# adaLN weights requested by ScalarE's queue instead of GpSimd's

## The chip, the cores and the metric

The kernel runs on one core of a Trainium2 chip. The metric is the device time of one execution in microseconds (us); the median of several runs is compared. The engines of the core are TensorE (PE, matmuls; its weight loads are PEld), VectorE (DVE), ScalarE (ACT), GpSimd (POOL) and SyncE (SP). A transfer (DMA) is requested by an instruction of one of these engines and carried by 16 DMA engines that all requests share.

## The reference

One layer of a decoder trunk, in fp32, for T = 320 tokens: 256 of a prompt and 64 of samples (8 sequences of 8 tokens), with 9 conditioning vectors c (one for the prompt, eight for the samples).

```python
mod = silu(c) @ w_ada + b_ada                       # (9, 6*2048): six sections
sh1, sc1, g1, sh2, sc2, g2 = split(mod, 6)
h = rmsnorm(x, norm1_g) * (1 + sc1) + sh1
p = h @ w_in                                        # q, k, v, og, u, ga, gb, alr
mix = gates(gla(q, k, v, alr, state_gla), pool(u, state_pool))
x = x + g1 * (mix @ w_o)
h2 = rmsnorm(x, norm2_g) * (1 + sc2) + sh2
x = x + g2 * ((silu(h2 @ w_gate) * (h2 @ w_up)) @ w_down)
y = rmsnorm(x, final_norm_g)                        # and new states of gla and pool
```

The adaLN part is the first line: w_ada has 2048 x 12288 fp32 values, 100 MB, and its results scale, shift and gate everything else.

## The kernel before, in words

Every large product is made of three matmuls on split operands (`mm3`, L171 to L173). SyncE loads raw weights in blocks of 512 KB (`raw_chunk`, tile raw, L149, three buffers), ScalarE makes the high part (`split`, tile whi, L157), VectorE the low part (wlo, L158); whi and wlo have four buffers each (WB = 4). Activations are split likewise into hh and hl.

w_ada isn't split. Its blocks are multiplied as they are by the transposed silu(c) (scT), in bursts of 32 or 16 matmuls; a burst's result is copied by ScalarE (tile adasb), transposed on TensorE and added up into mod by VectorE. The stages, in order of time:

- The head (0 to some 200 us). Sections 0 and 1 (shift and scale of h) in 16 blocks of 256 columns. `hada_load` (L225) requests such a block as two pieces of 1 MB into tile hraw (a pool with two buffers), `hada` (L236) is its burst, and the copy is L239. The products with w_in for the first head run in slices of rows between them (SLICES), since a slice needs only the rows of h that are ready. SyncE requests the first two blocks, GpSimd the other 14. Each block's reload waits for the burst that read its buffer two blocks earlier. GpSimd also requests xspill (transposed x put aside).
- The end of the head and the mixer (h = 0 to 3, to about 870 us). Sections 4, 2 and 3 in 24 blocks of the same size: `ada_load` takes the tile araw, `ada_piece` (L269) requests 1 MB, `ada_all` all pieces outstanding, `ada_burst` (L301, copy L310) multiplies. BURST_UNITS and LOAD_UNITS say after which projection of a head a burst or a request is written; araw has one buffer here, so a request waits for the burst before it. GpSimd also requests the states S (L775), writes o_gs (L811) and does small vector work. `anchor` makes a one-column copy (tick) on GpSimd behind which a request is put.
- w_o (some 870 to 1000 us). Eight pieces of section 5 are requested one at a time, each behind GpSimd's product xs (L1016).
- The FFN (to the end). Eight more pieces, requested by GpSimd.

Within an engine the instructions run in the order in which a scheduler placed them when the kernel was built; `high_priority` and `issue_after` are hints to it. `issue_after(x)` places an instruction behind x. The transfers that SyncE and ScalarE request use eight semaphores in turn, those of GpSimd eight others; a request that takes a semaphore waits until the transfer that had it before has landed.

Of the kernel before, what the change touches and what calls it, by code (L numbers as in the profile page):

```python
# [79 lines left out]
def body(tc, A):  # L80
# [57 lines left out]
    more = []  # L138
    last_raw = []
    last_mm = []  # L140

    def raw_chunk(src, nk, nn, pool=None, tag="raw", bufs=3):

# [8 lines left out]
    def split(raw):  # L152
        n = raw.shape[2]
        hi = wp.tile([P, 512 // n, n], F32R, tag="whi", bufs=WB, name=nm("whi"))
        lo = wp.tile([P, 512 // n, n], F32R, tag="wlo", bufs=WB, name=nm("wlo"))
        hi, lo = hi[:, 0:raw.shape[1]], lo[:, 0:raw.shape[1]]
        S.copy(hi, raw)  # L157
        V.tensor_sub(lo, raw, hi.bitcast(F32))  # L158
        return hi, lo

# [59 lines left out]
    def hada_load(sec, b0, pool, eng):  # L220
# [4 lines left out]
            eng.dma_start(t[:, k:k + 8], wada[:, k:k + 8, blk * P:(blk + 2) * P])  # L225
        return t

    def hada(sec, b0, t, pool):

        blk = sec * KT + b0  # L230
        w = 2 * P
        ps = misc()
        with tc.high_priority():
            for r in (3, 2, 1, 0):
                for j in range(4):
                    PE.matmul(ps[32 * j:32 * j + 32, 0:w], lhsT=scT[:, 4 * r + j, :], rhs=t[:, 4 * r + j, :],  # L236
                              start=r == 3, stop=r == 0, tile_position=(0, 32 * j))
        sb = pool.tile([P, w], F32, tag="adasb", name=nm("adasb"))
        S.copy(sb, ps[:, 0:w])  # L239
        pt = misc()  # L240
        for i in range(2):
            tr(pt[:, i * P:(i + 1) * P], sb[:, i * P:(i + 1) * P])
        dst = mod[:, blk:blk + 2, :]
        V.tensor_reduce(dst, pt[:, 0:w].rearrange("p (b j r) -> p b r j", b=2, j=4)[:, :, 0:9, :],
                        axis=AX.X, op=ALU.add)
        bb = bada[:, blk:blk + 2].unsqueeze(2).broadcast_to([P, 2, 9])
        V.tensor_tensor(dst, dst, bb, op=ALU.add)
        if sec == 1:
            V.scalar_tensor_tensor(dst, dst, 1.0, N1G[:, b0:b0 + 2].unsqueeze(2).broadcast_to([P, 2, 9]),
                                   op0=ALU.add, op1=ALU.mult)  # L250
# [8 lines left out]
    ada_want = []  # L259
    ada_ps = []  # L260

    def ada_piece(after=None):

        n, t, r = ada_want.pop(0)
        sec, b, nb, k0, nk = BURSTS[n]
        step = min(nk, 16 // nb)
        col = (sec * KT + b) * P
        with tc.issue_after(after) if after is not None else nullcontext():
            nc.gpsimd.dma_start(t[:, r:r + step], wada[:, k0 + r:k0 + r + step, col:col + nb * P])  # L269

    tick = cp.tile([P, 1], F32, name="tick")

    def anchor(src):

        return G.tensor_copy(tick, src).ins
# [5 lines left out]
            t = ada_raw[n] = apool[0].tile([P, nk, nb * P], F32, tag=tag, bufs=bufs, name=nm("araw"))  # L281
            ada_want.extend((n, t, r) for r in range(0, nk, min(nk, 16 // nb)))

    def ada_all(after=None):
        while ada_want:
            ada_piece(after)

    def ada_burst():

        n = len(ada_done)  # L290
        sec, b, nb, k0, nk = BURSTS[n]
        ada_done.append(n)
        w = nb * P
        if k0 == 0:
            ada_ps[:] = [misc()]
        ps = ada_ps[0]
        first = True
        with tc.high_priority(), tc.issue_after(last_mm[0]):
            for r in range(nk - 4, -1, -4):
                for j in range(4):  # L300
                    PE.matmul(ps[32 * j:32 * j + 32, 0:w], lhsT=scT[:, k0 + r + j, :], rhs=ada_raw[n][:, r + j, :],  # L301
                              start=k0 == 0 and first, stop=k0 + nk == KT and r == 0, tile_position=(0, 32 * j))
                first = False
        if k0 + nk < KT:
            return
        pt = misc()
        for q in range(0, nb, 2):
            wq = min(2, nb) * P
            sb = apool[0].tile([P, wq], F32, tag="adasb", name=nm("adasb"))
            S.copy(sb, ps[:, q * P:q * P + wq])  # L310
            for i in range(wq // P):
                tr(pt[:, (q + i) * P:(q + i + 1) * P], sb[:, i * P:(i + 1) * P])
        blk = sec * KT + b
        V.tensor_reduce(mod[:, blk:blk + nb, :], pt[:, 0:w].rearrange("p (b j r) -> p b r j", b=nb, j=4)[:, :, 0:9, :],
                        axis=AX.X, op=ALU.add)
        if b == KT - nb:
            dst = mod[:, sec * KT:(sec + 1) * KT, :]
            bb = bada[:, sec * KT:(sec + 1) * KT].unsqueeze(2).broadcast_to([P, KT, 9])
            V.tensor_tensor(dst, dst, bb, op=ALU.add)
            if sec == 4:  # L320
                V.tensor_scalar(dst, dst, 1.0, None, op0=ALU.add)
                V.tensor_tensor(dst, dst, N2G.unsqueeze(2).broadcast_to([P, KT, 9]), op=ALU.mult)

    def modp(sec, kt):
        return mod[:, sec * KT + kt, 0:1]
# [97 lines left out]
    with tc.tile_pool(name="head", bufs=1) as xp:  # L423
# [88 lines left out]
        def h_rows(b):  # L512

            def load(s):
                raws[s, b] = hada_load(s, b, xp, nc.gpsimd)
            return ([lambda: load(0), lambda: (h_pre(b), h_pre(b + 1)), lambda: load(1),
                     lambda: hada(0, b, raws.pop((0, b)), xp),
                     lambda: (hada(1, b, raws.pop((1, b)), xp), h_post(b), h_post(b + 1))])
# [7 lines left out]
        for si, (k0, k1) in enumerate(SLICES):  # L526
            last = k1 == KT
            bg = [] if last else [f for b in range(*SLICES[si + 1], 2) for f in h_rows(b)]
            if last:
                with tc.issue_after(spilt[-1]):  # L530
                    walr = xp.tile([P, KT, 16], F32, name="walr")
                    nc.gpsimd.dma_start(walr, win[:, :, OAL:OAL + 16])
                    nc.gpsimd.dma_start(msk, A["ci"])
                    cum = xp.tile([P, NM0 + NM1 + NMS], F32, name="cum")
                    nc.gpsimd.dma_start(cum, A["cf"][:, 64:CFW])
                    nc.gpsimd.dma_start(invc, A["cf"][:, 0:64])
            done = 0
            for ui, (kind, i, col) in enumerate(us):
                want = len(bg) * (ui + 1) // len(us)
                while done < want:  # L540
                    bg[done]()
                    done += 1
                if kind in "qku":
                    evac(proj(win, col, k0, k1, hh, hl), g0, kind, 0, 0 if si == 0 else 1)
                else:
                    for i, ps in enumerate(proj2(win, col, k0, k1, hh, hl)):
                        evac(ps, g0, kind, i, 0 if si == 0 else 1)
                if last and ui == 0:
                    alr_proj(walr, cum)
                if last and ui in (0, 1):  # L550
                    ada_load(ui, 2, "araw")
                    ada_all()
                if last and ui in (2, 3, 5, 6):
                    ada_burst()
                    if ui < 5:
                        ada_load(len(ada_done) + 1, 2, "araw")
                        ada_all()

    apool[0] = acx.enter_context(tc.tile_pool(name="ap", bufs=1, side="right"))

# [384 lines left out]
    for h in range(1, H):  # L945
        pump(RATE)
        g = new_group(h)
        for ui, (kind, i, col) in enumerate(units(h)):
            if kind == "og" and i == 0:
                pump(len(queue))  # L950
                new_gates(g)
            ps = proj(win, col, 0, KT, hh, hl)
            evac(ps, g, kind, i, None)
            if kind == "u":
                pump(len(queue))
                st, E = gla_steps(g)
                pst, psy = pool_steps(g)
                queue += pst + st
            if ui in BURST_UNITS[h]:
                ada_burst()  # L960
            if ui in LOAD_UNITS[h] and len(ada_done) < AMIX:
                ada_load(len(ada_done), 1)
                ada_all(None if ui in BURST_UNITS[h] else anchor((g.q if kind == "q" else g.og)[:, 0, 0:1]))
            pump(RATE)
        queue += psy + [merge_step(g, E)]
    pump(len(queue))
# [41 lines left out]
    for ui in range(8):  # L1008
        ps = proj(wo, 256 * ui, 0, KT, mh, ml, between=x1_rows)
        for i in range(2):  # L1010
            residual(ps, i, 2 * ui + i, 2)
            k = 2 * ui + i
            sq = sq_acc(acc, k, k == 0)
            if k == 12:
                exp_ln_set(sq)
            gi = G.tensor_tensor(s3(xs[:, k]), s3(x1[k][:, TP:T]), mods(4, k), op=ALU.mult).ins  # L1016
            if ada_want:
                ada_piece(gi)

    def rstd_bcast(acc):  # L1020
        pt = misc()
# [31 lines left out]
    for pi, (f0, f1) in enumerate(parts):  # L1053
        ah, al = {}, {}
        for f in range(f0, f1, 2):
# [14 lines left out]
            if pi == 0 and f >= 2:  # L1070
                if f in (4, 8, 12, 16):
                    ada_burst()
                if f in (2, 4, 8, 12):
                    ada_load(len(ada_done), 1)
                    ada_all()
        if pi == 0:
            bcx.close()
        else:
# [67 lines left out]
```

## Time and profile before

| | |
|---|---|
| median of 3 runs | 1975.34 us (1972.93 to 1976.12) |
| the profiled execution | 1972.99 us |
| its span (first to last instruction) | 1971.2 us |
| requests of hraw by GpSimd / SyncE | 28 / 4, 1 MB each, median 9.8 / 11.7 us to landing |
| requests of araw by GpSimd | 64, 1 MB each, median 8.7 us to landing |
| bytes by hardware queues / GpSimd's software queue | 261.81 MB / 136.57 MB |

The profile has a line per engine (busy us, share, instructions), a row of DMA shares in 40 slices of the span, queues with their packets and bytes, the chain of work that ended last, groups of instructions by line, and waits: "ACT whi L157 <- PE ps L172" is time in which ScalarE stood before the cast whi until TensorE's matmul into ps released it. An engine's wait costs only where TensorE, or whatever ends last, waits in turn.

### The profile page before, as it was taken

The page shows a single profiled execution, that of the slowest core. Times are in us where ns is not written, and L with a number is a line of the kernel's source. Part 1 is how long each engine was busy: PE and PEld are TensorE (multiplying, and loading weights), DVE is VectorE, ACT ScalarE, POOL GpSimd, SP SyncE. Part 2 cuts the span into 40 slices and gives each one's busy share as a digit, 9 for nine tenths or more (in the row PEclk, how much of TensorE's full clock was granted, in tenths as well). Part 3 has the DMA queues.
Part 4 walks back from the last instruction along what each step waited for, and adds up shares of the span by engine and source line. Part 5 has one row for each costly group of instructions (what it writes and reads, how often), then busy time and mean ns, then how long its engine had stood idle before and what let it go on. Part 6 is the DMA issues. An engine that isn't in the chain of part 4 may idle for free.

```text
span 1971.2 us, 34613 instructions
## 1 busy us (share of the span) xinstructions
PE 1924.5 (98%) x13808; PEld 1825.2 (93%) x13808; DVE 1007.0 (51%) x1935; ACT 826.9 (42%) x1485; POOL 207.3 (11%) x323
## 2 busy tenths in 40 slices
PE   5999999999999999999999999999999999999997
PEld 4889888988998899989989999999999999999997
DVE  3776454666355535665574444444444444444554
ACT  4433343544345433553354333333333434344443
POOL 2231131221121112111030000000000000000000
PEclk9999989999999999999999999999999999999998
DMA  9996647777875788579845555444545444444442
GB/s 349 354 354 237 203 150 264 219 230 251 256 223 188 247 268 272 183 249 321 269 153 158 186 188 182 145 150 144 156 145 155 150 150 150 150 151 144 149 139 98
DMA packets 287308, 400.60 MB, mean 203 GB/s; under 512 B 11953, under 2 KB 243921, under 8 KB 286809
## 3 DMA queue, kind: packets, MB, share of 16 engines
q1 hardware_dynamic: 250170, 261.81, 42.7%
q0 software_dynamic: 36976, 136.57, 19.5%
q8 instruction: 108, 1.77, 0.4%
q14 instruction: 54, 0.44, 0.1%
HBM read 373.90 MB, written 24.67 MB: 202 GB/s over the span
## 4 chain that ended last, share of the span: by engine, by line
PE 82%; DMA 3%; ACT 1%; DVE 0%; issue 0%; POOL 0%; ACTq 0%; DVEq 0%
PE ps L172 25%; PE ps L171 25%; PE ps L173 25%; PE pm L301 3%; PE pm L135 1%; DMA araw<-w_ada 1%; PE pm L786 1%; PE pm L807 1%; DMA raw<-w_o 1%; DMA S<-state_gla 1%; PE pm L752 1%; DMA o_gs<-S 0%; PE pm L782 0%; PE pm L591 0%; PE pm L741 0%; PE psy L171 0%
## 5 line engine op out<-in xcount | busy, mean ns | idle before, releaser
L158 DVE TENSOR_TENSOR wlo<-raw,whi 128x512 fp32r<-128x512 f32 x952 | 657.7, 694 | 792.4 <-ACT whi L157 779.9
L157 ACT CAST whi<-raw 128x512 fp32r<-128x512 f32 x952 | 587.8, 622 | 948.3 <-PE ps L172 830.1
L171 PE MATMUL ps<-hh,whi 128*128 128x320 f32 x1408 | 441.9, 314 | 6.1 <-ACT hh L337 2.6
L172 PE MATMUL ps<-hl,whi 128*128 128x320 f32 x1408 | 440.4, 313 | 0.0
L173 PE MATMUL ps<-hh,wlo 128*128 128x320 f32 x1408 | 437.4, 312 | 0.0
L172 PE MATMUL ps<-h2l,whi 128*128 128x320 f32 x1408 | 434.7, 309 | 0.0
L171 PE MATMUL ps<-h2h,whi 128*128 128x320 f32 x1408 | 434.7, 309 | 0.0
L173 PE MATMUL ps<-h2h,wlo 128*128 128x320 f32 x1408 | 434.2, 309 | 0.0
L171 PEld LDWEIGHTS ps<-hh,whi 128*128 128x128 f32 x1408 | 265.2, 188 | 19.7 <-issue 9.0
L172 PEld LDWEIGHTS ps<-hl,whi 128*128 128x128 f32 x1408 | 265.3, 188 | 10.4 <-issue 9.4
L173 PEld LDWEIGHTS ps<-hh,wlo 128*128 128x128 f32 x1408 | 264.7, 188 | 8.0 <-issue 5.3
L171 PEld LDWEIGHTS ps<-h2h,whi 128*128 128x128 f32 x1408 | 264.4, 188 | 3.4 <-ACT ah L337 3.4
L172 PEld LDWEIGHTS ps<-h2l,whi 128*128 128x128 f32 x1408 | 264.5, 188 | 0.1
L173 PEld LDWEIGHTS ps<-h2h,wlo 128*128 128x128 f32 x1408 | 264.5, 188 | 0.0
L171 PE MATMUL ps<-ah,whi 128*128 128x320 f32 x704 | 217.7, 309 | 0.0
L172 PE MATMUL ps<-al,whi 128*128 128x320 f32 x704 | 216.5, 308 | 0.0
L173 PE MATMUL ps<-ah,wlo 128*128 128x320 f32 x704 | 216.5, 308 | 0.0
L172 PEld LDWEIGHTS ps<-al,whi 128*128 128x128 f32 x704 | 132.0, 187 | 0.0
L171 PEld LDWEIGHTS ps<-ah,whi 128*128 128x128 f32 x704 | 131.9, 187 | 0.0
L173 PEld LDWEIGHTS ps<-ah,wlo 128*128 128x128 f32 x704 | 131.9, 187 | 0.0
L269 POOL DMA_DIRECT2D araw<-w_ada x64 | 55.1, 864 | 397.2 <-PE pm L301 385.9
L172 PE MATMUL ps<-ml,whi 128*128 128x320 f32 x256 | 79.3, 310 | 0.0
(282 smaller groups left out, 1634.2 us busy)
## 6 DMA issues: line engine op xcount, KB each, us to landing
raw<-w_gu SPq DMA_DIRECT2D x176, 512.0 KB, 3.5
raw<-w_in SPq DMA_DIRECT2D x170, 512.0 KB, 4.4
araw<-w_ada POOLq DMA_DIRECT2D x64, 1024.0 KB, 8.7
raw<-w_down SPq DMA_DIRECT2D x80, 512.0 KB, 3.5
hraw<-w_ada POOLq DMA_DIRECT2D x28, 1024.0 KB, 9.8
S<-state_gla POOLq DMA_DIRECT2D x16, 1024.0 KB, 8.3
o_gs<-S POOLq DMA_DIRECT2D x16, 1024.0 KB, 6.9
raw<-w_o SPq DMA_DIRECT2D x32, 512.0 KB, 6.2
```

The lines of the kernel that those rows point to most:

```text
L135: PE.transpose(out, in_, ident[:k, :k])
L157: S.copy(hi, raw)
L158: V.tensor_sub(lo, raw, hi.bitcast(F32))
L171: PE.matmul(ps, lhsT=whi, rhs=xhi, start=start, stop=False)
L172: PE.matmul(ps, lhsT=whi, rhs=xlo, start=False, stop=False)
L173: last_mm[:] = [PE.matmul(ps, lhsT=wlo, rhs=xhi, start=False, stop=stop).ins]
L269: nc.gpsimd.dma_start(t[:, r:r + step], wada[:, k0 + r:k0 + r + step, col:col + nb * P])
L301: PE.matmul(ps[32 * j:32 * j + 32, 0:w], lhsT=scT[:, k0 + r + j, :], rhs=ada_raw[n][:, r + j, :], start=k0 == 0 and first, stop=k0 + nk == ...
L752: PE.matmul(pt, lhsT=E["kdn"][:, s, d * P:(d + 1) * P], rhs=E["vn"][:, s], start=s == 0, stop=s == 1)
L786: PE.matmul(pt[32 * j:32 * j + 32, :], lhsT=qeP[:, d, 4 * gg + j, :], rhs=E["S0", gg, d][:, j], start=False, stop=d == 0, tile_position=(0 ...
L807: PE.matmul(pt, lhsT=E["kpn"][:, j, d * P:(d + 1) * P], rhs=E["vp"][:, gg], start=True, stop=True)
```

## The change

28 requests of hraw and 56 of araw go from GpSimd to ScalarE; the eight araw requests of the FFN stay. Each is placed behind an instruction of ScalarE: in the head behind the adasb copy of the last burst of the same section (`used`), in the mixer behind the adasb copy of the burst just written (`out`), or the last whi cast (`last_cast`) where no burst goes before, in w_o behind ScalarE's square sq. The four tick copies at those places are gone.

```diff
     def split(raw):
...
-        S.copy(hi, raw)
+        last_cast[:] = [S.copy(hi, raw).ins]
...
+    used = {}
     def hada(sec, b0, t, pool):
...
-        S.copy(sb, ps[:, 0:w])
+        used[sec] = S.copy(sb, ps[:, 0:w]).ins
...
-    def ada_piece(after=None):
+    def ada_piece(after=None, eng=nc.scalar):
...
-            nc.gpsimd.dma_start(t[:, r:r + step], wada[:, k0 + r:k0 + r + step, col:col + nb * P])
+            eng.dma_start(t[:, r:r + step], wada[:, k0 + r:k0 + r + step, col:col + nb * P])
...
-    def ada_all(after=None):
+    def ada_all(after=None, eng=nc.scalar):
         while ada_want:
-            ada_piece(after)
+            ada_piece(after, eng)
     def ada_burst():
...
-            S.copy(sb, ps[:, q * P:q * P + wq])
+            out = S.copy(sb, ps[:, q * P:q * P + wq]).ins
...
+        return out
...
             def load(s):
-                raws[s, b] = hada_load(s, b, xp, nc.gpsimd)
+                with tc.issue_after(used[s]):
+                    raws[s, b] = hada_load(s, b, xp, nc.scalar)
...
                 if last and ui in (0, 1):
                     ada_load(ui, 2, "araw")
-                    ada_all()
+                    ada_all(last_cast[0])
                 if last and ui in (2, 3, 5, 6):
-                    ada_burst()
+                    out = ada_burst()
                     if ui < 5:
                         ada_load(len(ada_done) + 1, 2, "araw")
-                        ada_all()
+                        ada_all(out)
...
+            out = last_cast[0]
             if ui in BURST_UNITS[h]:
-                ada_burst()
+                out = ada_burst()
             if ui in LOAD_UNITS[h] and len(ada_done) < AMIX:
                 ada_load(len(ada_done), 1)
-                ada_all(None if ui in BURST_UNITS[h] else anchor((g.q if kind == "q" else g.og)[:, 0, 0:1]))
+                ada_all(out)
...
-            gi = G.tensor_tensor(s3(xs[:, k]), s3(x1[k][:, TP:T]), mods(4, k), op=ALU.mult).ins
+            G.tensor_tensor(s3(xs[:, k]), s3(x1[k][:, TP:T]), mods(4, k), op=ALU.mult)
             if ada_want:
-                ada_piece(gi)
+                ada_piece(sq)
...
                     ada_load(len(ada_done), 1)
-                    ada_all()
+                    ada_all(None, nc.gpsimd)
```

The scheduler also moves other instructions. ScalarE at the start of the head, before (numbers in names count tiles in the order in which they are written; x2 is two instructions in a row):

```order
L239 COPY adasb_240<-pm_223 128x256
L157 CAST whi_285<-raw_283 128x512
L157 CAST whi_308<-raw_306 128x512
L157 CAST whi_346<-raw_344 128x512
L239 COPY adasb_264<-pm_247 128x256
L482 COPY xT_329<-pm_325 128x320
L482 COPY xT_338<-pm_334 128x320
L337 CAST hh_86<-xh_210 128x320
```

The same place now:

```order
L242 COPY adasb_240<-pm_223 128x256
L226 DMA hraw_302<-w_ada 128x8x256 x2
L158 CAST whi_285<-raw_283 128x512
L158 CAST whi_308<-raw_306 128x512
L158 CAST whi_346<-raw_344 128x512
L242 COPY adasb_264<-pm_247 128x256
L226 DMA hraw_403<-w_ada 128x8x256 x2
L486 COPY xT_329<-pm_325 128x320
L486 COPY xT_338<-pm_334 128x320
L341 CAST hh_86<-xh_210 128x320
```

A pair of requests stands behind each adasb copy, ahead of the casts that TensorE needs next. TensorE in the middle of the head, at the burst of the eleventh block (hraw_1356), before:

```order
L173 MATMUL ps_1001<-hh_91,wlo_1021 128x320
L236 MATMUL pm_1456<-hraw_1356,scT 32x256 x16
L171 MATMUL ps_1062<-hh_90,whi_1066 128x320
L172 MATMUL ps_1062<-hl_106,whi_1066 128x320
L173 MATMUL ps_1062<-hh_90,wlo_1067 128x320
```

The same burst now:

```order
L174 MATMUL ps_899<-hh_91,wlo_903 128x320
L135 MATMUL pm_1302<-cst,adasb_1300 128x128 x2
L135 MATMUL pm_1359<-cst,xn_132 128x128
L135 MATMUL pm_1359<-cst,xn_133 128x128
L135 MATMUL pm_1359<-cst,xn_134 128x128
L135 MATMUL pm_1368<-cst,xn_132 128x128
L135 MATMUL pm_1368<-cst,xn_133 128x128
L135 MATMUL pm_1368<-cst,xn_134 128x128
L239 MATMUL pm_1456<-hraw_1356,scT 32x256 x16
L172 MATMUL ps_937<-hh_90,whi_940 128x320
```

It stood behind the weights whi_1004 to whi_1021 and stands now ahead of whi_940: four blocks of w_in that were multiplied before it come after it. The burst before it (hraw_1234) stays ahead of whi_902 now, and the last of the head, hraw_1911, moved from the second half of whi_1629 to ahead of the second use of whi_1381. GpSimd in the last mixer stage, before:

```order
L811 DMA o_gs<-S_1004_6059 128x4x512
L269 DMA araw_6689<-w_ada 128x8x256 x2
L269 DMA araw_6995<-w_ada 128x8x256 x2
L269 DMA araw_7159<-w_ada 128x8x256 x2
...
L269 DMA araw_7868<-w_ada 128x8x256 x2
L275 COPY tick<-v_7377 128x1
L775 DMA S_1361_8224<-state_gla 128x4x512
L775 DMA S_1362_8226<-state_gla 128x4x512
```

and now:

```order
L816 DMA o_gs<-S_1003_6055 128x4x512
L816 DMA o_gs<-S_1004_6057 128x4x512
L278 COPY tick<-v_7374 128x1
L780 DMA S_1361_8221<-state_gla 128x4x512
L780 DMA S_1362_8223<-state_gla 128x4x512
```

The state loads no longer stand behind seven araw blocks, each of which waits for a burst.

More of the change, by code (lines that the diff above doesn't have):

```diff
@@ L140, in body @@
     last_mm = []
+    last_cast = []
     def raw_chunk(src, nk, nn, pool=None, tag="raw", bufs=3):
```

## The prediction

> **What bounds the kernel now.** I read the page's head first (who is busy), then the chain that ended last, then the busy time by stretches, and only then the waits.
>
> ```profile
> PE 1924.5 (98%) x13808; PEld 1825.2 (93%) x13808; DVE 1007.0 (51%) x1935; ACT 826.9 (42%) x1485; POOL 207.3 (11%) x323
> ...
> DMA  9996647777875788579845555444545444444442
> ...
> q1 hardware_dynamic: 250170, 261.81, 42.7%
> q0 software_dynamic: 36976, 136.57, 19.5%
> ...
> PE 82%; DMA 3%; ACT 1%; DVE 0%; issue 0%; POOL 0%; ACTq 0%; DVEq 0%
> ```
>
> TensorE (PE) is busy for 98% and fills 82% of the chain; DMA has 3% of it. The DMA row says where transfers could matter: the first three slices (0 to 148 us) are full, later ones mostly are not. The next view cuts the span into stretches; its columns are the stretch, busy us of PE, PEld, DVE, ACT and POOL (instructions in brackets), granted clock, DMA share, GB/s.
>
> ```profile
> 0.00:50.00 50.00, 28.25 (x251) 22.81 (x251) 15.32 (x46) 21.51 (x35) 12.86 (x22) 0.97 0.95 349
> 100.00:150.00 50.00, 48.99 (x430) 42.85 (x429) 37.37 (x85) 17.37 (x37) 16.23 (x22) 1.00 0.99 348
> 150.00:200.00 50.00, 48.51 (x343) 45.69 (x342) 28.01 (x53) 15.46 (x28) 4.66 (x8) 1.00 0.66 230
> 700.00:750.00 50.00, 50.00 (x417) 45.50 (x416) 18.58 (x36) 18.51 (x38) 8.33 (x11) 1.00 0.83 269
> 1550.00:1600.00 50.00, 50.00 (x343) 50.00 (x342) 21.88 (x33) 20.11 (x33) 0.00 (x0) 1.00 0.47 148
> 24.00:148.00 124.00, 117.18 (x1048) 100.01 (x1048) 83.01 (x195) 48.52 (x97) 35.85 (x47) 0.99 0.99 365
> 30.00:60.00 30.00, 27.52 (x240) 23.53 (x244) 15.96 (x42) 14.08 (x27) 7.66 (x10) 0.94 1.00 380
> ```
>
> The row at 1550 is TensorE undisturbed: 343 matmuls in 50 us, one each 0.146 us. Where the moved requests act, TensorE loses 21.75 us in the first 50 (start-up, ahead of any moved request but the first two), and then about 1 us in 50: 1.01 at 100, 1.49 at 150, none at 700. A change of the queue cannot win what TensorE does not lose; it can easily make it lose more. That asymmetry carries the forecast.
>
> **The waits the moved requests cause.** Columns: us in total, times, longest.
>
> ```profile
> ACT whi L157 <- PE ps L172: 830.1, 752, 4.7
> POOL araw L269 <- PE pm L301: 385.9, 21, 69.2
> ACT adasb L239 <- PE pm L236: 22.8, 12, 5.9
> POOL S L775 <- DMA o_gs<-S: 15.3, 7, 5.0
> PE pm L236 <- DMA hraw<-w_ada: 0.4, 1, 0.4
> PE pm L301 <- DMA araw<-w_ada: 1.0, 2, 0.5
> PEld pm L301 <- DMA araw<-w_ada: 1.5, 2, 0.8
> PE pm L786 <- DMA S<-state_gla: 0.6, 1, 0.6
> ```
>
> GpSimd (POOL) stands still 385.9 us in front of araw requests, but TensorE, which sets the end, waits only 0.4 us for hraw, 2.5 for araw and 0.6 for a state tile that is requested behind such araw rows: 3.5 us in all. If every one of them goes, that is -3.5; if a wait only changes its place, 0. I take -2.0, nearer to the upper end, since a request on ScalarE (ACT) no longer keeps the state loads waiting, while an araw tile is still released by the same burst of matmuls.
>
> **The issue cost.** How long the engine is held by one 1 MB request, in ns (least, median, most):
>
> ```profile
> L225 POOL DMA_DIRECT2D hraw<-w_ada x28: 882/892/905, 23.8 to 138.3; - x28
> L225 SPq DMA_DIRECT2D hraw<-w_ada x4: 576/3057/4450, 5.6 to 14.1; - x4
> L149 SPq DMA_DIRECT2D raw<-w_in x182: 367/368/2631, 16.9 to 857.3; - x182
> L157 ACT CAST whi<-raw 128x512 fp32r<-128x512 f32 x423 | 259.8, 623 | 412.9 <-PE ps L172 306.6 <-DMA raw<-w_in 36.9 <-DMA raw<-w_o 28.0
> ```
>
> 84 requests (28 hraw, 56 araw) leave GpSimd: 84 x 0.892 = 75 us there, on an engine that waits anyway, so 0. They arrive on ScalarE. No row shows a request of ScalarE, but SyncE (SP) made the same kind through a hardware queue: 0.368 us when the queue has room, 0.576 for the first of four 1 MB blocks, and up to 4.45 when the blocks before it are still in the queue. So 84 x 0.368 to 84 x 0.576 = 31 to 48 us of ScalarE. The last row above is the casts between 32 and 1000 us: ScalarE stood 306.6 us in front of them because TensorE had not yet freed a whi buffer. That is the cover, so 0 on the path. It ends where ScalarE is away longer than the lead of the four whi buffers, whose best witness is the longest of those waits, 4.7 us. A pair that costs 0.576 + 4.45 = 5.03 us overruns it by 0.3; if all 42 pairs did, +14. No such instruction can gain, so the ends are 0 and +14. A new pair meets at most what is left of one older pair in ScalarE's queue, where SyncE's slow ones met three earlier blocks, so I take +0.5. Behind a blocked request stand the casts and hh of the next rows; TensorE waits for those. SyncE's and GpSimd's own queues only get shorter neighbours: the xspill, state and o_gs requests left on GpSimd no longer stand behind 84 requests, which can only bring them forward. One wait is new on SyncE: its raw requests and ScalarE's share the eight semaphores of the hardware queues in turn, so about one raw request in six waits for an hraw or araw to land. In the built order the weights so held back are used 11 to 24 us of TensorE work after the very tile they wait for, so 0; without that distance TensorE would wait a raw's own landing. The four tick copies that drop, and the wait on the adasb copy (0.37 us, in program order on ScalarE itself) are at nothing beside these.
>
> **The request comes when the adasb copy is done,** not when the last matmul is. The row of adasb waits shows ScalarE already standing at that copy in 12 of the 16 head rows, so a request follows a burst by one copy, and 0.892 - 0.576 us of issuing is saved on each half. These cancel: 0.
>
> **The head's cadence** is the larger effect, and the diff doesn't tell it: the scheduler now puts the head's bursts earlier among the matmuls. Durations of one matmul and one burst of 32 (hada), and the last burst:
>
> ```profile
> 154.30 0.31 PE L171 MATMUL ps<-hh,whi 128*128 128x320 f32 x1
> 154.54 1.93 PE L236 MATMUL pm<-hraw,scT 128*32 128x256 f32 x32
> ```
>
> Counting the rows between bursts at 0.147 and 1.93 us, the time from the end of burst n to the start of n+2, in which that tile must be reloaded, was 14.7 to 18.2 us; now it is 11.2 to 16.5. The last burst stands 15.1 us earlier in TensorE's work, so it would start at 154.5 - 15.1 = 139.4, with 2.3 MB less of w_in used by then. The window 24 to 148 moved 365 GB/s x 124 us = 45.3 MB at a DMA share of 0.99; less 2.3 is 43.0 MB, wanted in 139.4 - 24 = 115.4 us: 373 GB/s. At the 365 of that row the transfers end 117.8 us after 24, 2.4 late; at the 380 of the window 30 to 60 they are in time; at the 348 of 100 to 150 they take 123.6 us, 8.2 late. I take +2.4, the row that covers the whole stretch, with ends 0 and +8.2. What is late next is nothing: after the last burst the DMA share falls to 0.66, so what is lost stays lost once and no more.
>
> **The last mixer stage** (h=3) is tighter by the same kind of move: from one burst's end to the next start 11.6 to 12.4 us before, 10.7 now, at a DMA share of 0.83.
>
> ```profile
> L269 POOL DMA_DIRECT2D araw<-w_ada x64: 748/882/987, 149.1 to 1216.4; - x64
> ...
> DMA to landing us min/median/max: 5.8/8.7/11.8
> ```
>
> A pair needs its second request (0.58) and its landing: 9.3 us at the median, in time, and 12.4 at the worst, 1.7 late on six reloads. Ends 0 and +10; I take +0.5, near the median row. Elsewhere in the mixer and in w_o the gaps are 20 us and more or the pieces come singly: 0, with the same landing row as cover.
>
> **Sum:** -2.0 + 0.5 + 0 + 2.4 + 0.5 = +1.4 us. The profiled execution took 1972.99 us (span 1971.2 and 1.8 around it), so 1974.4 by it; it stood 2.35 under the median of 1975.34, so the forecast for the median is 1976.7.
>
> The Trainium skill, "DMA: Bandwidth & Descriptors", section "Issuing engines are not separate DMA queues", speaks against any large gain: transfers from whichever engine share the same 16 DMA engines, and issuing from several saves only sequencer time. The trace agrees as far as it goes, since both queues together fill 0.99 of the DMA share in the head. By the rule alone the sum would be that of the issue term and the waits, between -3.5 and +0.5.
>
> **Rivals.** *Faster:* all 3.5 us of waits go, and so does the 1.49 us TensorE lost between 150 and 200, because the last hraw is out of the way earlier; the head keeps 373 GB/s or more. -5.0: 1970.3. For it: the faster issue. Against: the head's row of 365.
>
> *Slower, the head becomes bound by transfers.* A software packet carried 136.57 MB / 36976 = 3.7 KB, a hardware one 261.81 / 250170 = 1.05 KB. With hraw cut as small as the weights, hraw loses its larger share against raw, or the total rate falls. It decides below 373 GB/s over 24 to 139 us; it costs more than 0.2% (3.95 us) of the kernel below 352 with the other terms at -1.0 (43.0 MB / 0.352 = 122.2, 6.8 late); at 348 it is 8.2 late, and with the pairs in h=3 late by 1 us each on top, 1981.5 to 1986. For it: a share of 0.99 leaves no room, and the reload gaps shrink to 11.2 us against a landing of up to 14.7:
>
> ```profile
> DMA to landing us min/median/max: 7.1/10.2/14.7
> ```
>
> Against: raw landings were the late ones in the head (36.9 us of ScalarE's waits), and they would improve. The Trainium skill, same page, section "Queues, rings and completion order", has each DMA engine take turns between the queue rows packet by packet, by which a queue with smaller packets gets a smaller part; the packet sizes above are this trace's only evidence on it.
>
> *Slower, ScalarE is held by a full queue:* the +14 above, 1989. Against: at most one older pair is in that queue.
>
> *Nothing happens:* the transfers are hidden before and after, and the bursts' earlier places cost nothing: 1975.3.
>
> **From cases to numbers.** The sum as worked out 0.37, nothing 0.14, faster 0.13, head bound by transfers 0.26, ScalarE held 0.10. About 0.2%, 3.95 us, is what a measurement can tell from no change: the first two are within it, the third is faster, both slow cases are slower: 0.13, 0.51, 0.36. The range leaves out some of the fastest end and the queue-held case: 1970.5 to 1986.5. The likeliest case alone has 1973 to 1979.
>
> **What would show it.** Right: rows of ScalarE's hraw and araw requests at 0.37 to 0.6 us, TensorE's waits for araw gone, its idle time between 50 and 150 us up by 2 or 3 us with hraw as releaser. Wrong: such requests above 3 us, whi waits that end in a DMA request rather than in TensorE, a DMA rate in the head under 350 GB/s, or TensorE's idle time falling where no wait stood.

## The result and the profile after

The changed kernel takes 1993.1 us (median of 4 runs, 1991.1 to 1998.1) against 1975.67: a ratio of 1.0092, 95% interval 1.0079 to 1.0106, or 17.4 us slower by the medians (18.2 by the ratio). The forecast was 1976.7 within 1970.5 to 1986.5. The profiled execution has a span of 1991.2 us, 20.0 more than before.

The head of the page after, with the lines that answer to those of before:

```profile
PE 1925.9 (97%) x13808; PEld 1825.3 (92%) x13808; DVE 1010.2 (51%) x1935; ACT 827.8 (42%) x1485; POOL 133.2 (7%) x235
...
q1 hardware_dynamic: 250170, 261.81, 42.4%
q10 hardware_dynamic: 83264, 88.09, 13.2%
q0 software_dynamic: 14128, 48.49, 6.8%
```

The work is the same: 1925.9 us of TensorE against 1924.5, the same megabytes. ScalarE's queue is the new q10, in packets of 88.09 MB / 83264 = 1.06 KB. So the time went into waits. The stretches after (columns as before):

```profile
100.00:150.00 50.00, 42.57 (x397) 34.85 (x397) 33.48 (x80) 15.65 (x34) 6.63 (x11) 1.00 0.99 341
150.00:200.00 50.00, 47.43 (x338) 45.53 (x338) 32.29 (x57) 17.13 (x29) 0.00 (x0) 1.00 0.54 161
24.00:148.00 124.00, 106.19 (x974) 87.58 (x966) 74.12 (x179) 43.49 (x90) 10.93 (x19) 0.96 1.00 347
30.00:60.00 30.00, 22.83 (x199) 18.82 (x198) 13.54 (x38) 11.93 (x24) 2.15 (x4) 0.83 1.00 355
```

Between 24 and 148 us TensorE does 106.19 us of work where it did 117.18: 11 us of the 20 are here. The DMA share is 1.00 (0.99 before), but the rate is 347 GB/s, not 365. The rows of the requests, the waits of TensorE that they bring, a wait of SyncE (SPq) and the last burst of the head:

```profile
L226 ACTq DMA_DIRECT2D hraw<-w_ada x28: 374/529/6405, 25.2 to 138.3; - x28
...
PE ps L172 <- ACT hh L341: 7.0, 1, 7.0
PE pm L304 <- DMA araw<-w_ada: 3.1, 2, 1.7
PE pm L239 <- DMA hraw<-w_ada: 3.0, 3, 1.7
PEld pm L304 <- DMA araw<-w_ada: 2.4, 2, 2.0
...
SPq L150 <- DMA hraw<-w_ada: 11.2, 3, 8.6
...
153.68 1.93 PE L239 MATMUL pm<-hraw,scT 128*32 128x256 f32 x32 [0.76 <-DMA hraw<-w_ada]
```

The median request takes 0.53 us, inside the 0.37 to 0.58 of the forecast, but one takes 6.4 and another 3.8. The last hraw request leaves at 138.3 us, to the tenth where it left before, although its burst stands 15 us earlier in TensorE's order. That burst is the last row: it starts at 153.68, where before it started at 154.54. Moved up 15.1 us in the order, it came 0.9 us sooner, and TensorE stood for the rest. The row above it is new: SyncE's requests for weights stand 11.2 us until an hraw has landed; before there was no such row.

To place the loss I added up, for each TensorE instruction, the time to the next start beyond the median of its kind in the kernel before (bursts, short products and stops of before leave a remainder there too, so only differences count). This count is worked out from the traces of one execution each; the times decide.

| count in us up to | 50 | 250 | 350 | 1000 |
|---|---|---|---|---|
| before | 16.0 | 51.3 | 67.6 | 119.9 |
| after | 20.4 | 61.9 | 83.6 | 140.3 |
| head alone on ScalarE | 20.7 | 64.2 | 79.7 | 134.7 |
| mixer and w_o alone | 15.9 | 50.0 | 69.8 | 126.3 |

### The profile page after: what moved, and what is told of

Same layout as the page of the kernel before. It is cut to its first block, busy times and chain, and to the rows that moved or that the text cites. A ratio compares the mean times of both kernels' runs of the same rounds, so it can differ in the third digit from the quotient of the medians.

```text
span 1991.2 us, 34608 instructions
## 1 busy us (share of the span) xinstructions
PE 1925.9 (97%) x13808; PEld 1825.3 (92%) x13808; DVE 1010.2 (51%) x1935; ACT 827.8 (42%) x1485; POOL 133.2 (7%) x235
## 3 DMA queue, kind: packets, MB, share of 16 engines
q10 hardware_dynamic: 83264, 88.09, 13.2%
## 4 chain that ended last, share of the span: by engine, by line
PE 80%; DMA 3%; ACT 1%; DVE 1%; issue 0%; POOL 0%; ACTq 0%; DVEq 0%; POOLq 0%
PE ps L173 24%; PE ps L172 24%; PE ps L174 24%; PE pm L304 2%; DMA araw<-w_ada 2%; PE pm L135 1%; PE pm L791 1%; PE pm L757 1%; PE pm L812 1%; DMA o_gs<-S 1%; PE pm L746 0%; PE pm L787 0%; PE pm L687 0%; PE pm L596 0%; ACT L106 0%
## 5 line engine op out<-in xcount | busy, mean ns | idle before, releaser
L174 PE MATMUL ps<-mh,wlo 128*128 128x320 f32 x256 | 79.3, 310 | 0.0
```

The lines of the kernel that those rows point to most:

```text
L174: last_mm[:] = [PE.matmul(ps, lhsT=wlo, rhs=xhi, start=False, stop=stop).ins]
```

## The experiments

Theory A: ScalarE is held by requests into its full queue. Theory B: the bursts' earlier places in the head want the transfers sooner than they come. Theory C came later, for the start. Microseconds below are the ratio's excess times 1975, each run against the kernel before as timed in the same session.

### The head alone, and the rest alone

```diff
 # head alone: the kernel before, and
-                raws[s, b] = hada_load(s, b, xp, nc.gpsimd)
+                with tc.issue_after(used[s]):
+                    raws[s, b] = hada_load(s, b, xp, nc.scalar)
 # rest alone: the changed kernel without these lines
```

> Only the head's 28 hraw requests on ScalarE; the mixer and w_o stay on GpSimd as before. By the count of matmul start gaps in the two traces the changed kernel loses 4.4 us by 50 us and 13.7 by 175 us. If the head is the place: +11 to +14 us against before. If the mixer is the place: +5 or less.

> Only the 56 araw requests of mixer and w_o on ScalarE; hraw stays on GpSimd. If the head is the place: +2 to +6 us. If the mixer's moved instructions cost as much as the head: +8 or more. If araw on ScalarE is as good as on GpSimd: within 2 us.

Measured: the head 1.0068 (1.0056 to 1.0080), +13.4 us; the rest 1.0032 (1.0020 to 1.0045), +6.3. Together 19.7 against 18.2 for the whole. The head is the larger part, and the rest isn't free.

### The bursts at before's places

```diff
+    PLACES = [None, None, 18, 53, 101, 125, 167, 215, 263, 299, 347, 395, 431, 479, 523, 570]
     def hada(sec, b0, t, pool):
+        place = PLACES.pop(0)
...
-        with tc.high_priority():
+        with tc.high_priority(), (tc.issue_after(every_mm[place]) if place else nullcontext()):
```

every_mm lists the matmuls of mm3 as they are written, and the numbers are those behind which each burst stood in the kernel before. TensorE's order in the head is then before's, except that the last two bursts stand 4 and 10 matmuls (0.6 and 1.5 us) later.

> Head on ScalarE as in the run of the head alone, but each burst of the head is held behind the matmul it followed before, so that TensorE's order in the head is before's. Theory A (ScalarE is held by requests into a full queue, 6.41 us at 28.75): the late start of the products stays, +5 to +9. Theory B (the bursts' earlier places want transfers sooner than they come): at most +2. Both at work: half of the head's loss.

Measured: 1.0013 (1.0003 to 1.0023), +2.6. The same requests by the same engine cost 13.4 us at the early places and 2.6 at the late ones. That is Theory B, although the long hold is still there:

```profile
28.31 6.67 ACTq L228 DMA_DIRECT2D hraw<-w_ada  x1
36.58 0.82 ACT L346 CAST hh<-xh 128x320 fp32r<-128x320 f32 x2 [0.76 <-DVE xh L353]
```

In this timeline of ScalarE the request holds the queue for 6.67 us, and hh, which TensorE's first product needs, comes at 36.58 instead of 31.76. So the hold delays the start, and yet the time is nearly before's. The next runs ask why.

### Half of each block by each engine

```diff
-            eng.dma_start(t[:, k:k + 8], wada[:, k:k + 8, blk * P:(blk + 2) * P])
+            (eng or (nc.scalar if k == 0 else nc.gpsimd)).dma_start(t[:, k:k + 8], wada[...])
```

> The changed kernel with the second 1 MB piece of each hraw block requested by GpSimd behind the same instruction, so that at most 2 MB of ScalarE's stand in its queue. Theory A: no request of ScalarE takes over 0.6 us in the head, first product back at 32 to 33 us, +3 to +6 against before (the rest is the mixer's). Theory B: the bursts stand between the places of before and of the changed kernel; +10 or more.

Measured: 1.0037 (1.0025 to 1.0050), +7.3; no request of ScalarE in the head took over 0.46 us. The rest alone costs +6.3, so the head costs about 1 here. It fits A better than B as I had put them, but both factors moved at once (the places lie between the two orders), so it tells them apart less well than the pair that follows.

### Hold and places as two factors

```diff
-            eng.dma_start(...)
+            (nc.gpsimd if (sec, b0, k) == (1, 2, 8) else eng).dma_start(...)
```

This gives the one request that held ScalarE to GpSimd, once with before's places and once with the early ones.

> The run with the bursts at before's places (+1.9 us), but the one 1 MB request that held ScalarE for 6.67 us at 28.31 (second piece of the second reload of the other section) is made by GpSimd. Theory A (the hold costs what the first product is late, 4.5 us by the count at 50 us): -4 to -1 against before. If the hold was covered: +1 to +3.

> The head alone on ScalarE with its own (earlier) places (+13.4 us), and the same one request made by GpSimd. With the run before this makes two factors: places and hold. Theory B (places cost most): +8 to +10. Theory A: +5 or less.

| head on ScalarE | with the hold | without it |
|---|---|---|
| before's places | +2.6 (1.0003 to 1.0023) | +4.7 (1.0011 to 1.0038) |
| early places | +13.4 (1.0056 to 1.0080) | +17.8 (1.0070 to 1.0109) |

The places cost 11 to 13 us in either column. Removing the hold in this way gains nothing in either row, against Theory A. TensorE's timeline without the hold, at before's places, shows why:

```profile
32.38 0.90 PE L173 MATMUL ps<-hh,whi 128*128 128x320 f32 x2 [2.55 <-ACT hh L346]
41.88 1.51 PE L245 MATMUL pm<-hraw,scT 128*32 128x256 f32 x12 [5.39 <-DMA hraw<-w_ada]
```

The products start at 32.38, as before, and then TensorE stops 5.39 us for the first reloaded block. So the hold had hidden a transfer that was late as well. Not the whole stop was there before: the block landed at 41.74 us here, at 38.51 with the hold and at 34.97 in the kernel before, and here GpSimd's piece is under way at the same time. The section after next takes the hold away without that.

### The head's requests by SyncE

```diff
 # against the head alone
-                    raws[s, b] = hada_load(s, b, xp, nc.scalar)
+                    raws[s, b] = hada_load(s, b, xp, nc.sync)
```

> The head's 28 requests made by SyncE, behind the same instructions, so that TensorE's order is that of the head alone on ScalarE (earlier places) and ScalarE issues nothing. Theory B: +7 to +13, since the places are the cause whatever queue carries the blocks. If ScalarE's own time is the cause: within 3 us of before.

Measured: 1.0047 (1.0031 to 1.0064), +9.3. ScalarE issues nothing in the head and the early places still cost 9 us. This run has a wait of its own, though: SyncE stands before its hraw requests until a burst has freed the tile, with its raw requests behind. So how much of the 9.3 is the places' and how much of ScalarE's +13.4 its queue's is not shown. Its row of the window 24 to 148, waits of TensorE (60 to 200 us) and that wait of SyncE:

```profile
24.00:148.00 124.00, 110.26 (x996) 91.32 (x988) 77.70 (x187) 43.37 (x90) 12.84 (x21) 0.97 1.04 370
...
PE pm L238 <- DMA hraw<-w_ada: 4.6, 1, 4.6
PE ps L171 <- ACT whi L157: 3.5, 3, 2.2
PE ps L173 <- DVE wlo L158: 2.5, 4, 1.2
...
SPq L225 <- PE pm L238: 39.5, 12, 6.6
```

This run moved 370 GB/s with all blocks in one hardware queue; the changed kernel moved 347 with two, the head alone 351, in packets of the same size. From 100 to 150 us the head alone and this run are level (362 and 361), so a lower rate of ScalarE's queue as such is not shown. The waits of TensorE are divided between hraw and the casts of late raw blocks: the transfers as a whole are behind.

### The first reload ahead of the weights

```diff
-            eng.dma_start(...)
+            (nc.sync if (sec, b0) == (0, 2) else eng).dma_start(...)     # first run
+            (nc.gpsimd if b0 == 2 else eng).dma_start(...)               # second run
```

> The bursts at before's places, head on ScalarE, but the first reload (2 MB, tile used by the third burst) requested by SyncE, ahead of the w_in blocks in the same queue. It landed at 34.97 us when GpSimd asked for it, at 34.5 when SyncE did, at 38.3 to 41.7 when ScalarE did. Theory C (in a queue of its own with packets as small as the weights', the first reload shares with w_in and lands late; the hold and the wait for it are two faces of that): first product back at 32 to 33 us, no wait for hraw over 1 us, -4 to -1 against before. Theory A' (ScalarE's first requests cost in any case): +1 to +3, as with the bursts at before's places.

> As the run before, but both first reloads (4 MB) are requested by GpSimd as in the kernel before, the other 24 by ScalarE. Theory C: start as before; the count of matmul gaps from 50 to 225 us was 2 us less with ScalarE's requests at before's places, so -3 to 0 against before. Theory A': the same as before or above it.

Measured: 1.0015 (1.0001 to 1.0029), +3.0, and 1.0010 (0.9996 to 1.0025), +2.0. The trace bears the mechanism of Theory C out and the price doesn't. In the first of the two the block lands at 36.65 us, and

```profile
28.57 0.60 ACTq L228 DMA_DIRECT2D hraw<-w_ada  x1
32.04 0.82 ACT L346 CAST hh<-xh 128x320 fp32r<-128x320 f32 x2 [1.58 <-DVE xh L353]
```

the hold is gone, hh is back at 32.04, and of the waits for hraw in the start 0.5 us is left. The count up to 50 us falls from 20.5 to 18.1, to 250 from 53.8 to 52.2. But the times do not separate these two from the +2.6 of before's places with the hold, and neither is faster than before. So the hold's price, if it has one, is below what the runs can tell.

### Half the bytes at both sets of places

```diff
-        for k in range(0, KT, 8):
+        for k in (0, 8) if b0 == 0 else (0,):
...
-                    PE.matmul(..., rhs=t[:, 4 * r + j, :],
+                    PE.matmul(..., rhs=t[:, (4 * r + j) % (16 if b0 == 0 else 8), :],
```

> Head on ScalarE with the changed kernel's early places, but each reloaded block brings only its first 1 MB, which the burst uses twice (so the shift and scale of h are not the reference's): 14.7 MB less to move in the head, TensorE's work unchanged. Theory B1 (early places cost because the transfers are late): no more than 2 us slower than the run at the late places. Theory B2 (they cost by themselves, through what follows a burst): 6 us or more slower than that run.

> The same half of the bytes (shift and scale of h are not the reference's), bursts at before's places. Nothing is late and nothing held: -4 to 0 against before.

Both runs hold the bursts with a list PLACES as above, the first at the changed kernel's places (two of the sixteen, the eleventh and the fifteenth, came out 12 matmuls, 1.8 us, later than there).

Measured: early places 1.0009 (0.9999 to 1.0019), +1.8; late places 1.0000 (0.9988 to 1.0013), 0. The early places cost 11 us with all bytes and about 2 with half of them. So most of their price is that of late transfers. The window 100 to 150 of the two, early first:

```profile
100.00:150.00 50.00, 48.75 (x448) 41.73 (x446) 36.30 (x90) 18.07 (x36) 10.15 (x15) 1.00 0.88 288
...
100.00:150.00 50.00, 50.00 (x444) 44.14 (x437) 37.48 (x85) 19.16 (x38) 8.36 (x13) 1.00 0.78 246
```

With DMA shares of 0.88 and 0.78 TensorE is busy 48.75 and 50.00 us, where the changed kernel, at 0.99, had 42.57.

The start of the head's last burst tells the same over the runs that move the head alone and have the early places. In each of them 468 matmuls with w_in stand ahead of it (571 before), and the work that is left behind it is the same:

| early places, head requested by | last burst starts at, us | against half the bytes | price |
|---|---|---|---|
| ScalarE, half the bytes | 139.36 | 0 | +1.8 |
| SyncE | 149.26 | 9.9 | +9.3 |
| ScalarE (head alone) | 151.30 | 11.9 | +13.4 |
| ScalarE, one piece by GpSimd (without the hold) | 156.87 | 17.5 | +17.8 |

The starts are of one execution each. The price of the early places is about the time by which the last block is late.

### The mixer and w_o

```diff
 # first six blocks: mixer and w_o alone, and in ada_piece
+            (eng if (n < 6) == True and n < 24 else nc.gpsimd).dma_start(...)
 # mixer: mixer and w_o alone, w_o's pieces behind gi on GpSimd as before
 # w_o: the kernel before, its pieces behind sq on ScalarE
 # later blocks: the mixer's run, with the first six blocks requested as before
```

> Of the 56 araw requests only those of the first six blocks (12, all ahead of 450 us) on ScalarE; hraw, the later araw and w_o on GpSimd. In the run of mixer and w_o (+6.2 us) TensorE waits 2.6 and 0.9 us at 290 us in the first head's attention and runs some us at half clock behind. If that place is the mixer's loss: +3 to +5. If the later araw waits (2.9 us between 820 and 960) are: within 2 us.

> The mixer's 48 araw requests on ScalarE, hraw and w_o's eight as before. Of the +6.2 us of mixer and w_o, 2.9 were there by 350 us (moved instructions in the first head's attention at 290 us). If that is all the mixer costs: +3 to +4. If the araw waits of 2.9 us between 820 and 960 belong to the mixer's requests and not to w_o's: +6.

> Only w_o's eight requests on ScalarE, each behind its square. If they take DMA time from the last blocks of the mixer at a share of 0.95 to 1.0: +2 to +4. If the place is of no matter: within 1.5 us.

> In the mixer only the blocks from the seventh on (36 requests, after 450 us) on ScalarE; the first six, hraw and w_o as before. If the mixer's loss is the moved instructions at 290 us: within 2 us of before. If it is the waits for araw in the last mixer stage (6.6 us in the run of the whole mixer): +4 to +7.

Measured: first six blocks 1.0150 (1.0131 to 1.0169), +29.6; mixer 1.0050 (1.0033 to 1.0067), +9.9; w_o 0.9997 (0.9986 to 1.0009), -0.6; later blocks 1.0021 (1.0012 to 1.0030), +4.1.

W_o's requests cost nothing that the runs can tell. The later blocks cost 4.1, and their trace shows waits for araw; the row of their run, 300 to 1000 us, where the kernel before had 1.0 in two waits:

```profile
PE pm L304 <- DMA araw<-w_ada: 9.5, 6, 3.8
```

These are more than the price, so not each of them makes the kernel longer. What is left for the first six blocks is not well measured: some 6 us of the mixer's 9.9, but 2 of the 6.3 that mixer and w_o cost together. The trace of mixer and w_o shows 3.5 us of it, in the first head's attention:

```profile
290.02 1.09 PE L135 MATMUL pm<-cst,vTP 128*128 128x128 f32 x8 [0.89 <-ACT EX L630]
293.74 0.30 PE L135 MATMUL pm<-cst,w 128*128 128x128 f32 x1 [2.63 <-DVE w L657]
```

No transfer ends these waits. The scheduler moved the block's requests and its burst, and w_in matmuls that had lain between the transposes now stand elsewhere; before, the same wait was 0.3 us. The pauses are followed by matmuls 267 ns apart instead of 147 for about 2 us; the clock granted between 296 and 298 us is 0.50, against 1.00 before. That the burst's move made the other matmuls move is read from the orders, not tried by itself.

The run of the first six blocks cannot be read as a total. Its loss up to 350 us is that of mixer and w_o, but at 895 us it has one of its own, which neither theory spoke of:

```profile
894.83 5.20 POOL L272 DMA_DIRECT2D araw<-w_ada  x7
...
903.86 21.52 SPq L150 DMA_DIRECT2D raw<-w_o  x3
...
ACT whi L158 <- DMA raw<-w_o: 27.2, 3, 19.5
```

GpSimd makes seven requests in a row there, w_o's pieces among them, SyncE gets three raw blocks out in 21.5 us, and ScalarE stands up to 19.5 us for one. I take the bunched requests for the cause, but that wasn't tried.

### The parts added up

```diff
 # the changed kernel, and the PLACES of above
```

> The whole change with the head's bursts held at before's places. If the parts add up: the head at these places +2 to +3, mixer and w_o +6 to +10: +7 to +12 against before, 5 to 10 us under the changed kernel.

Measured: 1.0049 (1.0035 to 1.0064), +9.7 us, against 2.6 for the head at these places and 6.3 for the rest: 8.9. The whole change with nothing but the bursts put back costs about half of what it cost: 18.2 falls to 9.7.

## Why the prediction was wrong, point by point

**The bound** was read rightly: a kernel whose TensorE loses 1 us in 50 has little to win here. What was wrong is the size of the loss.

**The head's cadence** is the term that failed. It was +2.4 with ends 0 and +8.2; the pairs of runs measure 11 to 13. The place was right: the last burst was to be wanted at 139.4, and with half the bytes it started at 139.36. That the price is about the last block's lateness fits the table above. What failed is when that block would have landed. The sum had it at 141.8, 2.4 us late; in the changed kernel the burst started at 153.68, 14.3 late. Two terms of the balance were off. The rate was 347 GB/s and not 365, which alone makes 43.0 / 0.347 = 123.9 us after 24, 8.5 late. And the bytes: from 24 us on 43.0 MB had come by 148, but the last block was not among them whole, and when its burst started 347 x 129.7 = 45.0 MB had come. A balance of all bytes says when they could all be there, not when one block is, while others share the DMA engines. The rate alone is not the answer, as SyncE's run shows: at its 370 GB/s the same sum gives 0.8 late, and it was 9.9. Why the rate fell is open; TensorE stood more and asked for less, or the queue is slower, and no run parts the two. The slower rival, "bound by transfers", had mechanism and place right; it had 0.26, and its price stopped at 1986, with the same 43.0 MB in it.

**The held queue.** I took +0.5, and thought that a pair meets at most one older pair. The second reload's last piece met three older megabytes, 3.6 us after the first, and held ScalarE 6.4 us. The end of +14 was wrong the other way: no run shows a price of the hold, and the first reload came 3 to 7 us later than before, so that TensorE would have stood for that. The Trainium skill, "DMA: Bandwidth & Descriptors", section "Queues, rings and completion order", has the DMA engines take turns between queue rows by packets. The landings at the start agree with it, though no run shows the turns themselves: the first reload's last piece landed at 34.97 us in GpSimd's queue, with packets of 3.7 KB on average, at 34.5 and 36.7 ahead of the weights in SyncE's, and at 38.3 to 41.7 from ScalarE's queue with packets as small as the weights'. The issue cost itself was near: the 84 requests took 55 us of ScalarE with the holds, not 31 to 48, and the hraw ones 0.53 us at the median.

**SyncE's new wait**, put at 0, is there: 11.2 us in three waits until an hraw landed, up to 8.6. With the bursts at before's places one such wait of 9.0 us is left and the run costs 2.6, so by itself it isn't the 11 to 13. What it adds at the early places, where late weights stop TensorE too (2.0 us in front of whi from 50 to 165 us), no run shows.

**The waits that were to go**, -2.0: they grew. On matmuls alone, TensorE's waits for hraw went from 0.4 to 3.0 us and those for araw from 1.0 to 3.1. Only the state's 0.6 went. The 2.5 for araw in the sum was a misreading: the rows of PE and PEld show the same two stops, at 477 and 676 us, so it was 1.5 at most, and the 3.5 in all was 2.5.

**The last mixer stage**, +0.5 with ends 0 and +10: the later blocks, of which that stage is a part, cost +4.1. Of the 9.5 us of waits in their run 3.4 stand between 675 and 753 us, where the term sat, and 5.3 at 881 and 914 us, where I had put nothing. A median landing was the wrong row for a tile with one buffer: in that run araw's landings have a median of 8.5 us and go up to 13.7.

**The rest of the mixer and w_o**, 0: right for w_o (-0.6), wrong for the mixer. That the attention's matmuls had moved too was in the order, and I had compared only the bursts.

**The Trainium skill's rule on shared engines** ("DMA: Bandwidth & Descriptors", section "Issuing engines are not separate DMA queues") was right in its warning and wrong as a price: by it alone the sum ended between -3.5 and +0.5, since a change of the issuing engine saves only sequencer time; here the new queue came with other packets (1.06 KB for 3.7), other landings and another order of the scheduler, and +17.4.

No version tried beats the kernel before; w_o's requests on ScalarE are within what the runs can tell.

## What to carry to other kernels

Where DMA is full, moving an instruction up in the order need not bring its transfer sooner: the last burst moved up 15.1 us and came 0.9 us sooner. So ask when the last piece of each tile can land, with all that shares the DMA engines, and not when the sum of the bytes would fit at the rate of before. Before believing an issue-engine change, compare the built order of every engine that sets the end, not only of the engine that issues; here the moved bursts and matmuls cost more than the requests did. And where a long wait vanishes in an experiment without a gain, look at what the engine that sets the end waits for next.

## What the runs showed of the hardware that I had not expected

With DMA full and packets of about 1 KB in all weights' queues, 24 to 148 us moved 370 GB/s when SyncE's queue carried everything of w_in and hraw, and 347 to 356 when hraw had ScalarE's queue. Part of that may be lower demand while TensorE waited: from 100 to 150 us the head alone and SyncE's run moved 362 and 361. With the bursts at before's places, where TensorE hardly waited after 40 us, the row was this:

```profile
24.00:148.00 124.00, 113.55 (x1010) 97.51 (x1007) 79.49 (x187) 46.15 (x93) 8.12 (x15) 0.96 1.02 356
```

A request made when some 3 MB were outstanding in its own queue held ScalarE 5.7 to 6.7 us at the start of four kernels, against 0.53 at the median.
